# A hybrid gMLP and Mamba-2 block: transfers re-queued, PSUM split three and five, scan output normalised later, inverse roots four tiles at a time

## The chip, the core and the metric

The kernel runs on one core of one Trainium2 chip. Its engines work in parallel, each through its own instructions in order: TensorE (PE: matmuls and transposes), VectorE (DVE), ScalarE (ACT), GpSimd (POOL), and SyncE (SP), which here does nothing but issue DMA transfers, so that its instruction stream is one queue of transfers: one that waits holds up all behind it. The metric is the device time of a run in microseconds; lower is better.

## What is computed

One layer over 2048 latent tokens of width 1024 with 256 context tokens. All is fp32. Cut to what matters:

```python
def _rms(x):
    return x * rsqrt(mean(x * x, -1) + EPS)

def _token_mixer(h, ...):
    proj = h @ w_in                                   # u, v (1024 each), z (1024), xbc (1536), dt (32)
    xbc = silu(conv_centred(xbc)); xs, bm, cm = split(xbc)
    y = chunked_scan_forward(xs, dt, bm, cm) + chunked_scan_backward(...)   # chunks of 128 tokens
    y = y + xs * d_skip
    g = (y * silu(z)).reshape(b, l, 2, 512)
    ssd_out = _rms(g).reshape(b, l, 1024) * ssd_norm_w        # 2 groups
    u, v = split(gelu(proj[..., :2048]))
    v = _rms(v.reshape(b, l, 8, 128)) * gm_norm_w             # 8 heads
    mixed = einsum('hts,bcshd->bcthd', gm_ws, v) + gm_bs      # 128 x 128 per head and chunk
    return concat([u * mixed, ssd_out]) @ w_out

x = x + g1 * token_mixer(modulate(_rms(x) * norm1_w))
x = x + g2 * swiglu(modulate(_rms(x) * norm2_w))
return _rms(x) * final_norm_w
```

## The kernel before

Every large matmul is made of three, from operands split in a rounded high part and the low rest (mm3, L224 to L232). A unit is 24 such matmuls of 512 columns (8 slices of the inner dimension) into one PSUM buffer; there are 8 buffers of 512 fp32 columns, four in the pool psm (mmp, for units) and four in pss (smp, for all else).

The stages: modulation and the xbc projection of tokens 1024 to 2047 (block 1), then its v, u and z projections; the xbc projection of block 0; then, from about 750 us on, one long run of two streams. Its main stream is proj_z(0), proj_v(0), proj_u(0) (16 units each), then four output halves out_half (16 units each: block 1 with the gMLP half, block 0 with it, block 0 with the scan half, block 1 with the scan half). Its side stream is the backward scan's states of block 0 (ssd_bwd) and then ssd_y, the scan's output: 32 items, a chunk and a group each. For an item, y_load fetches a record (L687, two buffers of pool recp), y_seg the decay rows from fscr (L722, L723) and makes two masked matrices with ACT (L728, L730), DVE (L729, L731) and POOL (L733), y_out does the matmuls into three smp buffers (L750, L751, L753), a fourth for the state (L761), the sums on DVE (L756 to L767) with POOL's L766, multiplies by z (L771) and squares (L772). y_norm makes the inverse root of a chunk's two sums (newton, L238 to L243, 12 DVE instructions with L777, on 2 columns) and scales both halves on ACT (L780); y_store transposes them on PE (L787), copies (L789) and writes them to sscr. The function run takes SIDE = 2.74 steps of the side stream for one of the main stream, and a scheduler then sets the order of each engine from data, buffers and the written order. The last output half runs beside border, which prepares the feed-forward's operands: it reads x2scr (L1010), writes parts to cscr (L1020) and loads them back (L1044).

In the main stream proj_v makes gelu (gelu2: ACT L574, DVE L575, ACT L576, DVE L577), for each unit the inverse roots of its 4 heads (newton on 4 columns, with L635) and scales v (L637); mixing multiplies 4 units of v by gm_ws (L615), adds the bias (L617) and writes mscr (L620). proj_u multiplies gelu of u by that and writes gmscr (L602). out_half adds a unit to the residual (DVE L850), which it loads after the unit's matmuls (L849) from xT or x2scr and writes to x2scr at once (L851). load_mix loads operands of out_half, gmscr (L826) or sscr (L829), and splits them with ACT (L832) and DVE (L833). Weights come through L213 and are split by ACT (L216) and DVE (L217). The tiles tma (14) serve most of these, on both streams.

## Time and profile before

| what | value |
|---|---|
| median of 3 runs | 2999.11 us (2996.86 to 3005.99) |
| the profiled execution | 3001.86 us |
| its span, first to last instruction | 2999.7 us |
| PE busy | 2827.3 us, 94% |
| DVE, ACT, POOL busy | 2002.9, 1295.7, 633.1 us |
| mean granted clock of PE | 0.970 |
| DMA | 525.94 MB, mean 175 GB/s |

The profile is of one execution. Busy times are sums of instructions; a wait is put down to the engine and line that released it. The granted clock is a share of full speed: 1.0 is 2.4 GHz, 0.5 is 1.2 GHz, the two levels between which PE's clock changes here, so a value between is a mixture over the stretch.

### The profile page before, as it was taken

What the parts mean: (1) busy time and instruction counts of PE and PEld (TensorE: products, weight loads), DVE (VectorE), ACT (ScalarE), POOL (GpSimd) and SP (SyncE); (2) the same over time, 40 slices, a digit from 0 to 9 for tenths busy, and PEclk for the clock granted to TensorE, in tenths of its full rate; (3) what the DMA queues carried; (4) which work ended last, traced back from release to release, by engine and by line L of the source; (5) the groups of instructions that cost most, each with busy time, mean ns of one, the idle gap of its engine ahead of it and who ended that gap; (6) DMA issues with size and microseconds to landing.
All of it is one profiled execution on the core that took longest, in us unless ns stands there. A gap on an engine that the chain in (4) does not pass through costs nothing. (4 is left out here: it accounts for less than half of the span.)

```text
span 2999.7 us, 37193 instructions
## 1 busy us (share of the span) xinstructions
PE 2827.3 (94%) x12474; PEld 2253.5 (75%) x12474; DVE 2002.9 (67%) x3412; ACT 1295.7 (43%) x2387; POOL 633.1 (21%) x550
## 2 busy tenths in 40 slices
PE   7999999999998988999888799999999899999997
PEld 2788778878676767777767588888778788888885
DVE  6777966886788889778764555555776544445555
ACT  4444343344355556445452533333554333333443
POOL 3100000210131223222202244444110322221000
PEclk8999999999999999999999899999999999999998
DMA  5222567732754668877756544445766433224664
GB/s 222 88 91 88 186 217 231 261 120 82 231 168 148 194 203 254 242 244 235 210 163 221 172 158 159 160 158 165 256 224 206 142 106 106 96 100 131 226 193 157
DMA packets 295531, 525.94 MB, mean 175 GB/s; under 512 B 28838, under 2 KB 89638, under 8 KB 295340
## 3 DMA queue, kind: packets, MB, share of 16 engines
q1 hardware_dynamic: 295340, 523.57, 54.4%
q8 instruction: 98, 1.61, 0.2%
q14 instruction: 93, 0.76, 0.1%
HBM read 380.84 MB, written 142.62 MB: 175 GB/s over the span
## 5 line engine op out<-in xcount | busy, mean ns | idle before, releaser
L979 DVE TENSOR_TENSOR hl<-w,hl 128x1024 fp32r<-128x1024 f32 x286 | 371.9, 1306 | 308.9 <-ACT hl L978 127.1
L978 ACT CAST hl<-w 128x1024 fp32r<-128x1024 f32 x286 | 298.3, 1049 | 427.4 <-PE mmp L1094 121.5
L230 PE MATMUL mmp<-actt,whi 128*128 128x512 f32 x1120 | 458.2, 409 | 14.4 <-DVE t L850 8.0
L231 PE MATMUL mmp<-actt,whi 128*128 128x512 f32 x1120 | 448.5, 400 | 0.0
L232 PE MATMUL mmp<-actt,wlo 128*128 128x512 f32 x1120 | 445.8, 398 | 0.0
L1093 PE MATMUL mmp<-hl,hl 128*128 128x512 f32 x704 | 276.2, 392 | 5.5 <-DVE t L1201 2.3
L1095 PE MATMUL mmp<-hl,hl 128*128 128x512 f32 x704 | 276.0, 392 | 0.5 <-DVE hl L979 0.5
L1094 PE MATMUL mmp<-hl,hl 128*128 128x512 f32 x704 | 275.8, 392 | 0.0
L230 PEld LDWEIGHTS mmp<-actt,whi 128*128 128x128 f32 x1120 | 216.4, 193 | 65.9 <-DVE t L850 10.5
L231 PEld LDWEIGHTS mmp<-actt,whi 128*128 128x128 f32 x1120 | 216.4, 193 | 48.5 <-issue 5.5
L232 PEld LDWEIGHTS mmp<-actt,wlo 128*128 128x128 f32 x1120 | 215.6, 193 | 47.8 <-issue 1.7
L1093 PE MATMUL smp<-hl,hl 128*128 128x512 f32 x528 | 210.1, 398 | 16.5 <-ACT hl L978 16.5
L230 PE MATMUL mmp<-whi,actt 128*128 128x512 f32 x512 | 211.8, 414 | 0.0
L1094 PE MATMUL smp<-hl,hl 128*128 128x512 f32 x528 | 208.9, 396 | 0.0
L1095 PE MATMUL smp<-hl,hl 128*128 128x512 f32 x528 | 207.4, 393 | 0.0
L232 PE MATMUL mmp<-whi,actt 128*128 128x512 f32 x512 | 207.2, 405 | 0.0
L231 PE MATMUL mmp<-wlo,actt 128*128 128x512 f32 x512 | 205.8, 402 | 0.0
L985 DVE TENSOR_TENSOR t<-smp,t 128x512 f32<-128x512 f32 x88 | 60.5, 688 | 187.8 <-PE smp L1095 146.5
L1093 PEld LDWEIGHTS mmp<-hl,hl 128*128 128x128 f32 x704 | 132.4, 188 | 36.1 <-issue 2.7
L452 DVE SCALAR_TENSOR_TENSOR tma<-xin,cw,tma 128x512 f32<-128x512 f32 x192 | 144.3, 751 | 21.5 <-ACT tma L450 15.9
L985 POOL TENSOR_TENSOR w<-w 128x512 f32<-128x512 f32 x44 | 58.6, 1333 | 458.5 <-DVE hl L979 316.9
L733 POOL TENSOR_TENSOR tma<-tma 128x512 f32<-128x512 f32 x64 | 87.4, 1366 | 318.9 <-ACT tma L732 222.4
(267 smaller groups left out, 5875.7 us busy)
## 6 DMA issues: line engine op xcount, KB each, us to landing
w<-in_wall_dram SPq DMA_DIRECT2D x110, 512.0 KB, 4.1
ws<-in_wall_dram SPq DMA_DIRECT2D x104, 512.0 KB, 4.4
ascr<-t SPq DMA_DIRECT2D x154, 256.0 KB, 4.0
w<-ascr SPq DMA_DIRECT2D x154, 256.0 KB, 2.8
tma<-fscr SPq DMA_DIRECT2D x128, 256.0 KB, 5.8
w<-wscr SPq DMA_DIRECT2D x88, 256.0 KB, 3.5
t<-x2scr SPq DMA_DIRECT2D x74, 256.0 KB, 4.6
w<-in_wall_dram SPq DMA_DIRECT2D x66, 256.0 KB, 3.6
```

What stands on the lines that cost most here:

```text
L230: PE.matmul(ps, lhsT=lh, rhs=rh, start=(i == 0), stop=False)
L231: PE.matmul(ps, lhsT=lh, rhs=rl, start=False, stop=False)
L232: PE.matmul(ps, lhsT=ll, rhs=rh, start=False, stop=(i == n - 1))
L452: V.scalar_tensor_tensor(out=acc[:, :n], in0=raw[:, j:j + n], scalar=cw[:, ch, j:j + 1], in1=acc[:, :n], op0=ALU.mult, op1=ALU.add)
L733: G.tensor_tensor(out=A, in0=A, in1=fb, op=ALU.mult)
L978: S.copy(hi, x)
L979: eng.tensor_tensor(out=lo, in0=x, in1=hi.bitcast(F32), op=ALU.subtract)
L985: eng.tensor_tensor(out=o, in0=a, in1=b, op=ALU.add)
L1093: PE.matmul(ps, lhsT=hi[:, ms_], rhs=t[:, 0, :], start=first and k == 0, stop=False, skip_group_check=not first)
L1094: PE.matmul(ps, lhsT=hi[:, ms_], rhs=t[:, 1, :], start=False, stop=False, skip_group_check=not first)
L1095: PE.matmul(ps, lhsT=lo[:, ms_], rhs=t[:, 0, :], start=False, stop=k == 3, skip_group_check=not first)
```

## The change

Five things are changed together.

- *Transfer queue.* Writes of z, mixed v, u times v, and x2 are noted (behind) and issued only once the next unit's matmuls have been written (flush). out_half loads the residual tile of a unit while it writes out the one before. ssd_y asks for the record of item i + 2 before y_seg of item i + 1, from three buffers (rp3 is new), and for hscr at the head of y_seg, for group 1 into a tile of its own (hbp). The room for these comes from constants that are closed after the last xbc projection (cs2) and from NT2B, 3 to 2 (tiles of the second feed-forward matmul).
- *PSUM.* psm has three buffers and pss five; in ffn2 the first four banks are three mmp and one smp.
- *Scan output.* y_store transposes and writes the raw product, one item after y_out made it. y_rstd makes the inverse roots of four chunks and both groups at once (8 columns), transposes them and writes them to r3scr. load_mix loads them as rows over all partitions, and multiplies each of the 8 tiles by the norm weight and the row on DVE before the split.
- *v.* The inverse roots of four units are made at once (16 columns), and the four tiles are scaled then; mixing of the four before comes after the third unit instead of the second.
- *Feed-forward start.* Both inverse roots of block 1's residual are made at t = 1 of the first feed-forward stage; one was made within the last output half, one at t = 0. SIDE is 2.61; the side stream has 12 steps less.

The core of the diff:

```diff
-NT2B = 3
+NT2B = 2
+NPM = 3
-SIDE = 2.74
+SIDE = 2.61
...
-    psm = ctx.enter_context(tc.tile_pool(name="psm", bufs=4, space=PSUM))
-    pss = ctx.enter_context(tc.tile_pool(name="pss", bufs=4, space=PSUM))
+    psm = ctx.enter_context(tc.tile_pool(name="psm", bufs=NPM, space=PSUM))
+    pss = ctx.enter_context(tc.tile_pool(name="pss", bufs=8 - NPM, space=PSUM))
...
+    def behind(dst, src):
+        pending.append((dst, src))
+
+    def flush():
+        for dst, src in pending:
+            DMA.dma_start(dst, src)
+        pending.clear()
...
                     mm3(ps, [(hi[:, k * P:(k + 1) * P], lo[:, k * P:(k + 1) * P], hs[j][k][:, 0, :], hs[j][k][:, 1, :]) for k in range(KT)])
+                    flush()
                     t = gelu2(ps, tmp)
...
-                    DMA.dma_start(gmscr[h0 + i][:, ts_], t[:, :TB])
+                    behind(gmscr[h0 + i][:, ts_], t[:, :TB])
...
+                ms = sml()[:, :16]
                 for c in range(4):
...
-                    V.tensor_scalar(out=ms, in0=ms, scalar1=1.0 / P, scalar2=4 * EPS, op0=ALU.mult, op1=ALU.add)
-                    r = newton(ms, 4)
+                    vh.append(v)
+                    if c == 2 and prev is not None:
+                        mixing(*prev)
+                    if c < 3:
+                        yield
+                V.tensor_scalar(out=ms, in0=ms, scalar1=1.0 / P, scalar2=4 * EPS, op0=ALU.mult, op1=ALU.add)
+                r = newton(ms, 16)
+                for c, v in enumerate(vh):
...
+        hb = hbp[0].tile([P, TB], F32, name="hb", tag="hb") if g else tma()[:, :TB]
+        DMA.dma_start(hb, hscr[c][:, g * TB:(g + 1) * TB])
+        st["hb"] = hb
...
-        r = newton(ms, 2)
-        for g in range(2):
-            S.activation(ys[g], ys[g], AF.Copy, scale=r[:, g:g + 1])
+        r = newton(ms, 8)
         yield
...
+        ps = smp()
+        PE.transpose(out=ps[0:8, :P], in_=r, identity=ident)
+        t = tma()
+        S.copy(t[0:8, :P], ps[0:8, :P])
+        DMA.dma_start(r3scr[tb].rearrange("g (c x) -> (g c) x", x=P), t[0:8, :P])
...
+            if i + 2 < len(its):
+                st[i + 2] = y_load(rp, i + 2, *its[i + 2])
             if i + 1 < len(its):
                 yield from y_seg(st[i + 1], *its[i + 1])
...
+            if store is not None:
                 yield from y_store(*store)
...
+        if half == 1:
+            rb = [load_rb(r3scr[tb][g:g + 1, :], tma) for g in range(2)]
...
+                V.scalar_tensor_tensor(out=t[:, :TB], in0=t[:, :TB], scalar=sn, in1=rb[k // 4][:, :TB], op0=ALU.mult, op1=ALU.mult)
+                a = actt()
+                S.copy(a[:, 0, :], t[:, :TB])
+                V.tensor_tensor(out=a[:, 1, :], in0=t[:, :TB], in1=a[:, 0, :].bitcast(F32), op=ALU.subtract)
...
-                    t = tmp()
-                    DMA.dma_start(t[:, :TB], xT[m * P:(m + 1) * P, ts_] if half == 0 else x2scr[m][:, ts_])
+                    t = nxt.pop(0)
+                    if todo:
+                        fetch(*todo.pop(0))
+                    flush()
                     V.scalar_tensor_tensor(out=t[:, :TB], in0=ps, scalar=m_sb[:, 16 + m, 0:1], in1=t[:, :TB], op0=ALU.mult, op1=ALU.add)
-                    DMA.dma_start(x2scr[m][:, ts_], t[:, :TB])
+                    behind(x2scr[m][:, ts_], t[:, :TB])
```

What stands in the engines' orders at three places, before and after. In these rows a name carries the number of its buffer, and lines are those of the kernel that the rows are of.

PE in the u projection, before, from the end of a unit: the two transposes of a chunk (L787), then the matmuls of the next item (L750 to L761).

```order
L231 MATMUL mmp_10028<-actt_4807,whi_9442 128x512
L787 MATMUL smp_9788<-ident_225,tma_9350 128x128 x4
L787 MATMUL smp_9796<-ident_225,tma_9526 128x128 x4
L750 MATMUL smp_10003<-h01_2647,rec_sb_9609 128x512
L751 MATMUL smp_10004<-tma_9659,rec_sb_9609 128x512
L753 MATMUL smp_10002<-rec_sb_9609,tma_9615 128x64 x4
L753 MATMUL smp_10002<-rec_sb_9609,tma_9638 128x64 x4
L761 MATMUL smp_10018<-tma_9657,rec_sb_9609 128x512
```

After, in the output halves: the state's matmul of an item (L787), one transpose of the item before (L806), the next unit.

```order
L235 MATMUL mmp_10345<-actt_9536,whi_9653 128x512
L236 MATMUL mmp_10345<-actt_9536,wlo_9654 128x512
L787 MATMUL smp_10374<-tma_10139,rec_sb_9847 128x512
L806 MATMUL smp_10386<-ident_232,tma_10184 128x128 x4
L234 MATMUL mmp_10394<-actt_9501,whi_9937 128x512
L235 MATMUL mmp_10394<-actt_9501,whi_9937 128x512
L236 MATMUL mmp_10394<-actt_9501,wlo_9938 128x512
```

The transposes stood in pairs, on tiles that ACT had scaled; they stand singly now, on tiles that DVE wrote.

DVE in the u projection, before: L575 and L577 are the two gelu steps that read a unit's PSUM buffer (mmp), L601 the product with v, L238 to L243 the inverse root, L756 to L765 the scan's sums.

```order
L575 SCALAR_TENSOR_TENSOR tma_9688<-tma_9688,mmp_9663 128x512
L238 TENSOR_SCALAR sml_9696<-sml_9336 128x2
L756 TENSOR_TENSOR tma_9725<-smp_9713,eac_474 128x512
L239 TENSOR_SCALAR sml_9696<-sml_9696 128x2
L575 SCALAR_TENSOR_TENSOR tma_9775<-tma_9775,mmp_9750 128x512
L577 SCALAR_TENSOR_TENSOR tma_9688<-tma_9688,mmp_9663 128x512
L241 TENSOR_TENSOR sml_9697<-sml_9696 128x2
L764 TENSOR_TENSOR tma_9725<-tma_9725,tma_9511 128x512
L601 TENSOR_TENSOR tma_9688<-tma_9688,tma_9661 128x512
L242 SCALAR_TENSOR_TENSOR sml_9697<-sml_9697,sml_9336 128x2
L765 TENSOR_TENSOR tma_9725<-tma_9725,smp_9712 128x512
L243 SCALAR_TENSOR_TENSOR sml_9696<-sml_9697,sml_9696 128x2
```

After: gelu is L590 and L592, the product L617, the scan's sums L782 to L793, its matrices L758, a weight's low part L221.

```order
L590 SCALAR_TENSOR_TENSOR tma_9131<-tma_9131,mmp_9105 128x512
L758 SCALAR_TENSOR_TENSOR tma_9078<-tma_9078,acs_479,tma_9079 128x128
L782 TENSOR_TENSOR tma_9150<-smp_9138,eac_481 128x512
L758 SCALAR_TENSOR_TENSOR tma_9078<-tma_9078,acs_479,tma_9079 128x128 x3
L592 SCALAR_TENSOR_TENSOR tma_9131<-tma_9131,mmp_9105 128x512
L789 TENSOR_TENSOR h01_2607<-h01_2607,smp_9153 128x512
L617 TENSOR_TENSOR tma_9131<-tma_9131,tma_9103 128x512
L790 TENSOR_TENSOR tma_9150<-tma_9150,hb_8851 128x512
L590 SCALAR_TENSOR_TENSOR tma_9189<-tma_9189,mmp_9163 128x512
L791 TENSOR_TENSOR tma_9150<-tma_9150,smp_9137 128x512
L221 TENSOR_TENSOR wlo_9318<-ws_9315,whi_9317 128x1024
L793 TENSOR_TENSOR tma_9150<-tma_9150,hb_8851 128x512
```

Before, the second unit's first step (mmp_9750) stands ahead of the first unit's last (mmp_9663); after, a unit is done with before the next begins, and the narrow instructions are gone from between.

The SP queue in the last output half, before: the residual's load (L849), its write (L851), border's writes (L1020).

```order
L849 DMA t2_14188<-x2scr4_165 128x512
L1020 DMA cscr6_2_193<-t2_14153 128x512
L1020 DMA cscr7_2_201<-t2_14103 128x512
L851 DMA x2scr4_165<-t2_14188 128x512
L1020 DMA cscr4_2_209<-t2_14196 128x512
L849 DMA t2_14226<-x2scr5_166 128x512
L851 DMA x2scr5_166<-t2_14226 128x512
```

After: load L878, write L584, border's writes L1069, a weight L1104.

```order
L878 DMA t2_13653<-x2scr4_172 128x512
L584 DMA x2scr2_170<-t2_13567 128x512
L584 DMA x2scr3_171<-t2_13605 128x512
L1104 DMA w4_13911<-in_wall_dram 128x1024
L1069 DMA cscr3_2_212<-t2_13624 128x512
L1069 DMA cscr5_2_204<-t2_13664 128x512
L878 DMA t2_13701<-x2scr5_173 128x512
L1069 DMA cscr6_2_200<-t2_13666 128x512
L1069 DMA cscr7_2_208<-t2_13616 128x512
L1069 DMA cscr4_2_216<-t2_13709 128x512
L878 DMA t2_13739<-x2scr4_172 128x512
L584 DMA x2scr4_172<-t2_13653 128x512
```

Before, the load of a unit's tile stood behind the write of the unit before; after, it stands ahead of it, by one or two units.

## Rows read from the trace of the kernel before

**Rows 1.** The page, engine busy time and share of the span.

```profile
PE 2827.3 (94%) x12474; PEld 2253.5 (75%) x12474; DVE 2002.9 (67%) x3412; ACT 1295.7 (43%) x2387; POOL 633.1 (21%) x550
```

**Rows 2.** Windows, one row for each stretch named in the prediction.

```profile
core 0: us, PE busy (x) PEld busy (x) DVE busy (x) ACT busy (x) POOL busy (x), PEclk, DMA share, GB/s
860.00:1028.00 168.00, 148.72 (x701) 118.03 (x700) 148.42 (x444) 97.82 (x312) 35.74 (x30) 0.95 0.52 159
1028.00:1152.60 124.60, 111.76 (x502) 85.90 (x501) 100.89 (x219) 70.77 (x168) 38.71 (x29) 0.96 0.70 223
1152.60:1555.00 402.40, 369.31 (x1628) 290.23 (x1629) 305.35 (x640) 199.41 (x459) 95.37 (x79) 0.94 0.74 227
1555.00:1662.00 107.00, 94.54 (x375) 73.68 (x374) 51.68 (x74) 36.65 (x53) 17.05 (x11) 0.94 0.63 199
1662.00:1700.00 38.00, 19.35 (x63) 13.20 (x64) 25.82 (x33) 20.92 (x31) 8.97 (x7) 0.73 0.64 226
1700.00:2999.70 1299.70, 1263.81 (x5482) 1034.29 (x5481) 734.90 (x807) 502.85 (x640) 339.07 (x225) 0.99 0.49 160
```

**Rows 3.** Waits of PE, whole program: us in total, times, longest.

```profile
PE smp L787 <- ACT tma L780: 34.5, 9, 8.4
PE smp L1093 <- ACT hl L978: 16.5, 1, 16.5
PE mmp L230 <- DVE t L850: 8.0, 6, 3.0
PE smp L787 <- DVE tma L757: 5.5, 1, 5.5
```

**Rows 4.** The same wait in 1028 to 1152.6, then in 1152.6 to 1555.

```profile
PE smp L787 <- ACT tma L780: 6.6, 2, 4.9
PE smp L787 <- ACT tma L780: 19.8, 5, 8.4
```

**Rows 5.** Waits of ACT and of the SP queue in 795 to 1640.

```profile
ACT tma L728 <- DMA tma<-fscr: 126.2, 47, 7.2
...
SPq L687 <- POOL tma L766: 80.7, 24, 11.3
SPq L851 <- DVE tma L850: 66.6, 35, 5.6
```

**Rows 6.** DVE by line and shape; 128x4 in 860 to 1028, others 795 to 1640.

```profile
L243 DVE SCALAR_TENSOR_TENSOR sml<-sml 128x4 f32<-128x4 f32 x48 | 10.4, 217 | 0.7
...
L833 DVE SCALAR_TENSOR_TENSOR actt<-xin,vec,actt 128x512 fp32r<-128x512 f32 x32 | 22.6, 746 | 1.7 <-ACT actt L832 1.7
L242 DVE SCALAR_TENSOR_TENSOR sml<-sml 128x2 f32<-128x2 f32 x48 | 13.7, 286 | 0.7
```

**Rows 7.** Timeline of the last half: start us, us, engine, line.

```profile
1643.91 0.32 SPq L851 DMA_DIRECT2D x2scr<-t  x1
1645.48 0.45 SPq L849 DMA_DIRECT2D t<-x2scr  x1
1650.02 0.75 DVE L850 SCALAR_TENSOR_TENSOR t<-mmp,m_sb,t 128x512 f32<-128x512 f32 x1 [3.73 <-DMA t<-x2scr]
1650.80 0.32 SPq L851 DMA_DIRECT2D x2scr<-t  x1
```

**Rows 8.** Timeline at the feed-forward's start, queue and PE.

```profile
1679.14 0.33 SPq L851 DMA_DIRECT2D x2scr<-t  x1
...
1683.11 0.79 PE L1093 MATMUL smp<-hl,hl 128*128 128x512 f32 x1 [16.53 <-ACT hl L978]
```

**Rows 9.** Timeline of PE and DVE in the u projection.

```profile
1051.20 0.39 PE L230 MATMUL mmp<-actt,whi 128*128 128x512 f32 x1
1055.96 0.39 PE L230 MATMUL mmp<-actt,whi 128*128 128x512 f32 x1
1058.47 0.68 DVE L577 SCALAR_TENSOR_TENSOR tma<-tma,mmp 128x512 f32<-128x512 f32 x1
1059.20 0.50 PE L230 MATMUL mmp<-actt,whi 128*128 128x512 f32 x1 [2.40 <-DVE tma L577]
```

More of the change, by code (lines that the diff above doesn't have):

```diff
@@ L131 @@
     rscr = [tc.dram_tile([1, TB], F32, name=f"rscr{i}") for i in range(4)]
+    r3scr = [tc.dram_tile([2, TB], F32, name=f"r3scr{i}") for i in range(4)]
     r2scr = [tc.dram_tile([1, TB], F32, name=f"r2scr{i}") for i in range(4)]
@@ L394 @@
     tot = cst.tile([P, NT, 32], F32, name="tot")
-    halo = cst.tile([P, 12, 2], F32, name="halo")
+    halo = cs2.tile([P, 12, 2], F32, name="halo")
     def dt_block(c0, stat):
@@ L645, in proj_v @@
         yield
+    zdone = [0]
     def proj_z(blk, hs):
@@ L710, with y_load @@
     hv = lambda ap: bc(ap.rearrange("p (a o) -> p a o", o=1), HD)
-    def y_load(rp, c, g):
-        return {"rc": load_rec(rp, c, g, True)}
+    hbp = []
+    def y_load(pools, i, c, g):
+        return {"rc": load_rec(pools[i % 3 == 2], c, g, True)}
     def y_seg(st, c, g):
@@ L839, in out_half, with fetch @@
         pend = None
+        nxt = []
+        def fetch(m, j):
+            t = tmp()
+            ts_ = slice((blk * 2 + j) * TB, (blk * 2 + j + 1) * TB)
+            DMA.dma_start(t[:, :TB], xT[m * P:(m + 1) * P, ts_] if half == 0 else x2scr[m][:, ts_])
+            nxt.append(t)
+        todo = [(m0 + i, j) for m0 in range(0, 8, 2) for j in range(2) for i in range(2)]
+        fetch(*todo.pop(0))
         for m0 in range(0, 8, 2):
@@ L855, in out_half @@
                     if half == 1:
-                        acc[j] = sq_acc(acc[j], t[:, :TB], last_acc if last_acc and j == 1 and m == 0 else tmp)
+                        acc[j] = sq_acc(acc[j], t[:, :TB], last_acc if last_acc and m == 0 else tmp)
                         if m == 7:
                             pend = (acc[j], r2scr[blk * 2 + j], tmp)
-                            if j == 1:
-                                if last is None:
-                                    rstd_store(*pend)
-                                else:
-                                    last.append(pend)
+                            if last is not None:
+                                last.append(pend)
+                                pend = None
+                            elif j == 1:
+                                rstd_store(*pend)
                                 pend = None
@@ L959 @@
     late = []
-    accp = ctx.enter_context(tc.tile_pool(name="accp", bufs=1, reuse_waits="tile"))
+    accp = ctx.enter_context(tc.tile_pool(name="accp", bufs=2, reuse_waits="tile"))
     def acc1():
@@ L1165, in ffn1 @@
                 stage_y(t)
-            if blk == 0 and t == 0:
-                rstd_store(*box.pop())
+            if box and t == 1:
+                for b in box:
+                    rstd_store(*b)
+                box.clear()
             if blk == 0 and t % 2 == 1:
@@ L1214, in ffn2 @@
             if i == 0:
-                bank[p] = bank[1] if p in (6, 7, 4) else bank[5] if p == 3 else [mmp() if p == 1 else smp() for _ in range(4)]
+                bank[p] = bank[1] if p in (6, 7, 4) else bank[5] if p == 3 else [mmp() if p == 1 and m < NPM else smp() for m in range(4)]
             hi, lo = rdy.pop(n)
```

95 lines of the change are left out of this document (47 added, 48 removed).

## The prediction

> **What bounds the kernel now.** I read the page's engine shares first: TensorE (PE) is busy 2827.3 us of the span, 94% [rows 1], so time can only come from what is left to it: idle time, and time at a low clock. Then I cut the program where the changed code runs and read both per stretch [rows 2]. The edits lie in 860 to 1700 us; after 1700 PE is busy 1263.81 of 1299.7 us at clock 0.99 and little is to be had. For each stretch I take idle (length less PE busy) plus clock loss (length times one less the clock; a little too much, since it also counts time in which PE did nothing):
>
> - 860 to 1028, v projection (16 units of 24 matmuls): 19.3 + 8.4 = 27.7 us
> - 1028 to 1152.6, u projection (16 units): 12.8 + 5.0 = 17.8 us
> - 1152.6 to 1555, three output halves (48 units): 33.1 + 24.1 = 57.2 us
> - 1555 to 1662, the last output half (16 units): 12.5 + 6.4 = 18.9 us
> - 1662 to 1700, start of the feed-forward: 18.7 + 10.3 = 29.0 us
>
> Together 150.6 us. No edit that leaves PE's work alone can give more than about that here.
>
> Next, who is waited for [rows 3]. The largest wait is that of the transposes of the scan output (L787) for ACT's normalising copies (L780): 34.5 us in 9 waits. L787 also waits 5.5 us for DVE L757, which frees a PSUM buffer. Then 16.5 us once at the feed-forward's start, and 8.0 us for output buffers that DVE L850 has not yet freed. A gap costs twice: in the 38 us in which the wait of 16.53 us falls [rows 2, 8], the granted clock is 0.73, so PE ran part of it at the lower of its two levels, 1.2 instead of 2.4 GHz, after standing idle; in the last stretch, which has few gaps, it is 0.99. Last, why ACT is late: it waits 126.2 us for the rows of fscr, and the queue that loads them (SP, in order) stands 80.7 us before the record load L687, whose two buffers POOL still reads, and 66.6 us before the x2scr write L851, whose data DVE has not made [rows 5]. So the side stream is late because writes and a short pool hold up its loads, and PE, in order too, pays for it at L787.
>
> **The change part by part.** *Normalisation out of the scan.* Each of 16 chunks had a narrow inverse root on DVE and two copies on ACT (L780) before the two transposes. Now the transpose takes the raw product, and 4 inverse roots of 8 columns serve 4 chunks each. On PE's order the transpose of an item now stands behind the next item's matmuls, and its input is one DVE multiply, made a whole item earlier. The 34.5 us of waits for L780 lose their cause. What is late next at that place is DVE itself (L757, L756, h), and the fifth PSUM buffer of that pool takes most of it. On DVE the 128x2 rows [rows 6] with their siblings (six rows, 48 + 48 + 48 + 16 + 16 + 16 instructions) sum to 53.2 us; a quarter of the instructions is left, 13.3 us at the same duration, a saving of 40 us. In return load_mix gets one multiply for each of 32 tiles at L833's 0.746 us [rows 6]: 24 us more on DVE, in the stretch 1400 to 1700. Net 16 us less.
>
> *Four tiles of v at once.* The 128x4 rows [rows 6] with their siblings (six rows) sum to 37.7 us in 860 to 1028; a quarter is left, if 16 columns cost what 4 do, as 2 and 4 columns do (286 ns against 217 ns, no dearer for the wider): 28 us less of DVE's 148.4. The price: v's last multiplies come 4 units together, and mixing is moved one unit later, to cover that. This stretch is DVE's: 148.4 of 168 us [rows 2]. After it DVE has some 114 us (28 of v, 6 of the scan's share), PE's own floor is 168 - 27.7 = 140 us, and PE becomes the bound. I take **22 us** of 27.7. The v projection of the other block (before 779 us) has the same edit but PE stands hardly idle there: zero. The Trainium skill (Perfetto Trace Analysis, Optimizing Scalar/DVE Operations) says that every DVE instruction pays about 60 ns for data access on SBUF and that grouping helps a saturated engine. The narrow rows agree with it, at more than that figure; by 60 ns alone an estimate for the 144 instructions saved would be 9 us instead of 28, and the sum 5 to 10 us worse.
>
> *u projection.* L787's waits for L780 there are 6.6 us [rows 4] of the 12.8 idle; with the clock they caused I take **12 us** of 17.8, before the cost of the PSUM split, below.
>
> *Three output halves.* Most idle time there is L787's, 19.8 us for L780 alone [rows 4] of 33.1, and the largest of the rest is its 5.5 us for L757. Against taking all: DVE is busy 305.4 of 402.4 us and loses only about 5 net there; the floor of PE is 345 us, so DVE would stand at 87%, and some waits will come back as waits for DVE. I take **40 us** of 57.2.
>
> *Queue order.* Writes of z, v, u and x2 are held until the next unit's matmuls are written out, the residual tile is fetched a unit ahead, records have three buffers and are asked for an item earlier, hscr has a buffer of its own. In the last half this cuts a loop that the timeline shows [rows 7]: the write goes out at 1643.91, only then the next load at 1645.48, DVE L850 stands 3.73 us until it has landed, then the write at 1650.80. A turn is 6.9 us, a unit of PE's 24 matmuls 5.45 us (its first and last L230 stand at 1051.20 and 1055.96 [rows 9], seven turns of 0.68 us, and there are eight). Fetching ahead takes the load out of it. I take **12 us** of 18.9, and of the next stretch **15 us** of 29.0: PE stood 16.53 us until 1683.11 for a split of a tile that the queue loaded only behind the last write at 1679.14 [rows 8]; that write waited on the same loop. It will not vanish, since 12 loads still stand behind the last write. The cost: a held write keeps its tile a unit longer, and the fetch one more, out of the same 14 tiles; against that the scan keeps one product where it kept up to three. I price that at zero, 0 to 10 us.
>
> *PSUM three and five.* A unit may now start when the unit three before it is freed, not four. The bound: at 1059.20 PE waited 2.40 us for L577's release; the unit before had begun at 1051.20 [rows 9], and with three buffers it would have had to wait for the same release, 7.95 us. I went through PE's unit starts and DVE's releases from 803 us on: there are three such clumps in the u projection (8.8, 3.2 and 8 us at worst) and three in the output halves (4, 6 and 6.5 us), some 36 us; two smaller ones before 779 us make 44. At the other end it is zero: the lag arises since DVE takes two units at once (in DVE's order before, shown in the section on the change, the second unit's L575 stands ahead of the first's L577, with newton's instructions between), and the new order takes them one after the other. I take **20 us**, nearer the middle, since no row shows the new lag. The feed-forward's banks (three and one for the first four, then four) are as many as before: zero.
>
> *Rest.* NT2B 3 to 2 leaves 14 tiles for a peak that I count at 14: zero, 0 to 8 us. Both last inverse roots go to t = 1 of the feed-forward: 1 us, below what I can tell. The multiplies at the head of the last half stand before PE's first units: 8 of 0.75 us, **3 us**, 0 to 6.
>
> The sum: 22 + 12 + 40 + 12 + 15 = 101 gained, 20 + 3 lost: 78 us. The profiled execution took 3001.86 us, 2.8 over the median of the runs; 2999.1 - 78 gives **2921 us**.
>
> **The rivals.** *DVE takes over.* If the waits at L787 only move to DVE, which is 75 to 88% busy there, the gain is DVE's own saving and the queue's: 28 + 6 in the v and u stretches, half of the 40, and 20 at the end, less 23: 51 us, 2948; at worst 25 us, 2974. For it: rows 2. Against it: ACT's 126.2 us for fscr [rows 5] stand in front of DVE's L729 on the same tiles, so part of DVE's lateness is the queue's.
>
> *All of it.* Three buffers cost nothing and PE comes within 30 us of its floor: 2999 - 120 = 2879. For it: the even new order.
>
> *Slower: three PSUM buffers decide.* If DVE's lag behind PE stays what it was, 44 us of waits come, in gaps of up to 8 us, each with a low clock behind it: with half as much again, 66 us. It decides from the point at which the rest gives less than that; with L787's waits merely exchanged for it (gain 45 us): 3020. The Trainium skill (Perfetto Trace Analysis, Optimization Strategy) says that a gap that repeats on the engine that should be saturated can mean too few buffers. The two stalls on L577 with four buffers agree; by that rule taking one away makes it worse.
>
> *The change does not reach.* The queue's waits are exchanged for waits on free tiles and only the narrow DVE work goes: 2999 - 10 = 2989 to 2999.
>
> **How the numbers follow.** Forecast (2895 to 2945) 0.50; DVE takes over (2945 to 2988) 0.23; all of it (2860 to 2895) 0.14; does not reach (within 0.3%) 0.05; slower 0.08. A measurement of this kernel tells about 0.3% (9 us) from no change. So faster 0.87, same 0.05, slower 0.08. The range from 2872 to 2980 leaves out the upper end of the second case, the lower of the third, and the last two.
>
> **What would show it.** Right: L787's successor waits under 8 us in all; PE idle in the scan's stretches falls by half, the clock there to 0.98; the v stretch is about 20 us shorter; DVE L850's wait for x2scr is gone in the last half; the wait at the feed-forward's start is under 8 us. Wrong: waits of PE's main matmuls for the gelu's second DVE step or L850's successor above 30 us (three buffers), or DVE above 92% in the scan's stretches with PE still idle (DVE).

## The result and the profile after

The changed kernel takes 2977.35 us (median of 4 runs, 2974.7 to 2980.2), the kernel before 2997.99 beside it: a ratio of 0.9931, interval 0.9906 to 0.9956. That is 21 us less where 78 were forecast; the direction is right, the time lies at the upper end of the range, the size is off by more than three times.

In the profiled execution (2980.2 us, span 2978.4) the page has, against [rows 1]:

```profile
PE 2815.9 (95%) x12478; PEld 2252.8 (76%) x12478; DVE 1977.8 (66%) x3012; ACT 1272.8 (43%) x2360; POOL 637.6 (21%) x550
```

PE's idle time (span less busy) went from 172.4 to 162.5 us, its busy time fell by 11.4. To see where, both spans are cut at the same work in PE's own order: at the first matmul of block 0's z projection, at that of the last output half, at that of the feed-forward, and behind the feed-forward's first 96. Windows of the kernel before, then of the changed one (columns as in rows 2):

```profile
0.00:735.44 735.44, 699.26 (x3223) 548.59 (x3223) 546.59 (x1028) 316.51 (x608) 76.04 (x152) 0.98 0.50 161
735.44:1549.60 814.16, 744.96 (x3312) 579.20 (x3311) 639.17 (x1467) 413.94 (x1050) 191.97 (x156) 0.95 0.67 207
1549.60:1657.49 107.89, 96.61 (x388) 76.09 (x386) 52.11 (x76) 39.02 (x57) 17.05 (x11) 0.94 0.62 202
1657.49:1705.90 48.41, 28.58 (x100) 19.93 (x101) 30.80 (x38) 28.94 (x41) 13.02 (x9) 0.79 0.59 201
1705.90:2999.70 1293.80, 1257.91 (x5457) 1029.66 (x5455) 734.20 (x806) 497.31 (x634) 335.01 (x222) 0.99 0.49 161
```

```profile
0.00:738.28 738.28, 698.78 (x3222) 550.86 (x3222) 535.10 (x884) 317.52 (x608) 74.22 (x152) 0.98 0.49 160
738.28:1540.06 801.78, 739.52 (x3316) 577.26 (x3315) 609.26 (x1192) 387.86 (x1016) 198.61 (x156) 0.95 0.69 212
1540.06:1640.10 100.04, 90.41 (x388) 73.27 (x386) 69.23 (x98) 42.83 (x65) 18.31 (x12) 0.95 0.76 248
1640.10:1675.98 35.88, 24.55 (x98) 18.83 (x96) 28.03 (x33) 22.10 (x35) 11.67 (x8) 0.86 0.55 195
1675.98:2978.40 1302.42, 1262.62 (x5461) 1032.59 (x5459) 736.20 (x807) 502.44 (x638) 334.76 (x222) 0.98 0.49 160
```

The second rows are the scan's stages, that is the scan beside z, v, u and three output halves: 12.4 us shorter, PE idle 69.2 us before and 62.3 after, the clock 0.95 in both. Little of the forecast's main gain is there. The last half is 7.9 us shorter, the feed-forward's first 96 matmuls are 12.5 us shorter (idle 19.8 to 11.3, clock 0.79 to 0.86). The first row is 2.8 us longer and the last 8.6.

Within the second rows, v, u and the three output halves, before and after:

```profile
859.95:1006.08 146.13, 128.02 (x592) 102.05 (x590) 128.56 (x379) 86.72 (x278) 33.32 (x28) 0.94 0.48 146
1006.08:1152.56 146.48, 132.47 (x612) 101.88 (x610) 120.76 (x283) 81.87 (x201) 41.12 (x31) 0.97 0.71 226
1152.56:1549.60 397.04, 363.95 (x1605) 285.76 (x1605) 300.67 (x634) 194.60 (x453) 95.37 (x79) 0.94 0.74 226
```

```profile
864.91:1003.55 138.64, 125.79 (x597) 100.58 (x595) 106.24 (x236) 82.69 (x273) 31.98 (x27) 0.95 0.52 150
1003.55:1149.03 145.48, 130.49 (x616) 102.58 (x614) 119.25 (x230) 75.53 (x192) 42.87 (x33) 0.97 0.77 235
1149.03:1540.06 391.03, 361.70 (x1600) 283.53 (x1600) 291.46 (x566) 179.43 (x435) 101.84 (x79) 0.94 0.75 230
```

So v gives 7.5 us, u 1.0, the three halves 6.0, and z, the rest of the row, takes 2.1 us more.

Who PE waits for in 754 to 1566, the largest (us in total, times, longest), against [rows 3]:

```profile
PE smp L819 <- DVE sml L247: 22.9, 4, 8.3
PE smp L631 <- DMA gw<-in_gmw_dram: 13.2, 6, 6.2
PE mmp L234 <- DVE tma L592: 9.2, 2, 8.0
PE mmp L234 <- DVE tma L895: 8.7, 1, 8.7
PE smp L787 <- DVE h L789: 5.6, 1, 5.6
PE smp L779 <- POOL tma L762: 4.1, 2, 2.9
```

The 34.5 us for the normalising copies are gone, as forecast. In their place stand four waits of a new small transpose (L819) for the chain of inverse roots right ahead of it, which I overlooked; the mixing's weights (L631), 1.6 us before; main buffers, of which there are three (L234); and waits behind the load's bursts of VectorE steps (L787 once, and L895, below). At the feed-forward's start the largest wait is 8.24 us where [rows 8] had 16.53:

```profile
PE mmp L1144 <- DVE hl L1028: 9.3, 2, 8.2
```

And the side stream, against [rows 5]: ScalarE's wait for the broadcast row sums is nearly what it was. DVE, with 25 us less to do, waits longer behind ScalarE for the same loads (56.7 us in 38 before, at L729 for L728). The SyncE queue still stands before the held writes (the three last rows, whole program).

```profile
ACT tma L757 <- DMA tma<-fscr: 117.9, 44, 6.8
```

```profile
DVE tma L758 <- ACT tma L757: 74.0, 39, 5.7
```

```profile
SPq L584 <- DVE tma L895: 63.4, 19, 8.5
SPq L584 <- DVE tma L617: 60.8, 25, 9.8
SPq L584 <- DVE tma L679: 46.1, 18, 6.5
```

Single executions of one kernel differ here by 6 to 10 us, so a trace is read for its waits, and times are compared as ratios to the kernel before, measured beside each kernel.

### The profile page after: what moved, and what is told of

Same layout as the page of the kernel before. It is cut to its first block, busy times and chain, and to the rows that moved or that the text cites. A ratio compares the mean times of both kernels' runs of the same rounds, so it can differ in the third digit from the quotient of the medians.

```text
span 2978.4 us, 36719 instructions
## 1 busy us (share of the span) xinstructions
PE 2815.9 (95%) x12478; PEld 2252.8 (76%) x12478; DVE 1977.8 (66%) x3012; ACT 1272.8 (43%) x2360; POOL 637.6 (21%) x550
## 5 line engine op out<-in xcount | busy, mean ns | idle before, releaser
L234 PE MATMUL mmp<-actt,whi 128*128 128x512 f32 x1120 | 456.1, 407 | 24.9 <-DVE tma L592 15.4
L234 PEld LDWEIGHTS mmp<-actt,whi 128*128 128x128 f32 x1120 | 214.6, 192 | 74.9 <-DVE tma L592 17.6
L234 PE MATMUL mmp<-whi,actt 128*128 128x512 f32 x512 | 211.1, 412 | 2.4 <-DVE tma L679 2.4
L1144 PEld LDWEIGHTS mmp<-hl,hl 128*128 128x128 f32 x704 | 133.7, 190 | 38.9 <-DVE hl L1028 10.2
L1142 PEld LDWEIGHTS mmp<-hl,hl 128*128 128x128 f32 x704 | 133.5, 190 | 38.4 <-ACT t L1167 4.2
```

Source lines behind the costliest of these rows:

```text
L234: PE.matmul(ps, lhsT=lh, rhs=rh, start=(i == 0), stop=False)
L1142: PE.matmul(ps, lhsT=hi[:, ms_], rhs=t[:, 0, :], start=first and k == 0, stop=False, skip_group_check=not first)
L1144: PE.matmul(ps, lhsT=lo[:, ms_], rhs=t[:, 0, :], start=False, stop=k == 3, skip_group_check=not first)
```

## First experiments: the new waits one by one

Theory A: the forecast gain was given back in the new waits; each taken away brings its time. Theory B: something under them sets the pace, and a wait taken away comes back elsewhere.

**Late roots.** The roots' transpose stands after the next item's output and transposes.

```diff
-        r = newton(ms, 8)
-        yield
-        ps = smp()
-        PE.transpose(out=ps[0:8, :P], in_=r, identity=ident)
...
             if store is not None:
                 yield from y_store(*store)
+            if root is not None:
+                y_root(*root)
```

> The changed kernel with one thing moved: the transpose that turns the inverse roots of a token block (four times in the scan) is no longer issued right behind their chain of eleven small VectorE steps, but after the next item's output and transposes, some 20 us later. Theory A (the gain was given back in new PE waits): the four waits of the small transpose, 5.33, 5.86, 8.27 and 3.46 us, are gone, three of them certainly (the last token block's has least work left to hide it), nothing takes their place, and the stretches at the lower clock behind them are shorter: 2977 minus 18 to 30, so 2947 to 2959 us. Theory B (the scan's stages last as long as the side stream's chain of loads, ScalarE and VectorE steps lets them; PE's waits only move): the waits of that line go too, but PE waits elsewhere for VectorE or the side stream by as much: 2970 to 2980 us.

2970.84 us, 0.9919 (0.9905 to 0.9933): some 4 us, not told apart from the changed kernel. The waits of that line for the chain are nearly gone (1.1 us of 22.9); PE's waits on main buffers behind the load's burst rose:

```profile
PE mmp L234 <- DVE tma L903: 21.1, 3, 11.7
PE smp L631 <- DMA gw<-in_gmw_dram: 18.8, 8, 8.5
```

**PSUM four and four.** (The expectation calls the old wait the state product's; it was that of the transposes of the scan's output.)

```diff
-NPM = 3
+NPM = 4
```

> The changed kernel with four PSUM buffers for the main products and four for the scan's, as before the change, the rest as changed. Theory A: the waits for a main buffer (15.4 us in 4 at the gelu's second step, 8.7 us in 1 at the output's step) go, but the state product's wait of the kernel before (34.5 us in 9) comes back, since it stood on the fourth small buffer; balance 0 to +15 us, 2977 to 2992. If the normalisation step that held the small buffers is gone with the change anyhow, the wait does not come back and it gains 10 to 20 us: 2957 to 2967. Theory B (side stream decides): within 5 us, 2972 to 2982.

2979.23 us, 0.9945 (0.9930 to 0.9961): level with three and five. The main-buffer waits mostly go, and the transposes wait for buffers that DVE L782 frees, 16.5 us in 5.

**v tile by tile again.**

```diff
-                ms = sml()[:, :16]
...
+                    r = newton(ms, 4)
```

> The changed kernel with the inverse roots of v taken tile by tile again (four newton chains of 4 columns in place of one of 16, mixing behind the second tile), the rest as changed. Theory A: the grouping took some 13 us of small VectorE steps out of each v stage (two of them) without shortening it, since the mixing's loads came late and the last tile's chain now stands ahead of four multiplies; undoing it costs 0 to 8 us: 2977 to 2985. Theory B (VectorE's load decides in the scan's stages): the small steps are back, 12 to 26 us slower: 2989 to 3003.

2975.79 us, 0.9933 (0.9921 to 0.9945): nothing. The narrow steps are back on DVE (1336 instructions in the scan's stages for 1192) and the time is the same. In this trace v takes 146.97 us (138.64 with the grouping) and u 138.01 (145.48): what the grouping gains in v is lost again in u.

**Writes at once.**

```diff
     def behind(dst, src):
-        pending.append((dst, src))
+        DMA.dma_start(dst, src)
```

> The changed kernel with the writes of the main stream's results issued at once again (not behind the next product), the prefetch of the output's operand kept. Theory A: each write blocks the one DMA queue until its VectorE step is done, 1 to 4 us each, and with it the loads behind; what the reordered queue brought is 8 to 25 us, so 2985 to 3002 us. Theory B: the queue has slack, since PE waits mostly for VectorE: within 6 us, 2971 to 2983.

2988.81 us, 0.9980 (0.9968 to 0.9991): 15 us of the 21 hang on the held writes.

**The load's burst.** In the changed kernel DVE has this before the last half (start us, us):

```profile
1551.24 2.07 DVE L858 SCALAR_TENSOR_TENSOR xin<-xin,vec,tma 128x512 f32<-128x512 f32 x3
1553.22 1.89 DVE L861 TENSOR_TENSOR actt<-xin,actt 128x512 fp32r<-128x512 f32 x3
1555.03 0.74 DVE L895 SCALAR_TENSOR_TENSOR tma<-mmp,m_sb,tma 128x512 f32<-128x512 f32 x1
```

Rows like the first two stand without a gap from 1534.7 on, 20 us of them (16 multiplies and 16 differences), and only then comes L895, which frees a main buffer; PE stood 8.72 us for it. Taken in quarters between products:

```diff
-               early(out_half(0, 1, s0), 16, 2, lambda: [load_mix(2, 1), load_mix(3, 1)], s1)), 1),
+               early(out_half(0, 1, s0), 16, 4, quarters(2, 1, s1), None)), 1),
```

> The changed kernel with the mixers' operand loads (16 tiles ahead of each output half) taken in four quarters, one between each two products, instead of all 16 at one place; nothing else changed, and the last half's load begins four products ahead in place of two. In the changed kernel the 32 VectorE steps of such a load (16 multiplies of 0.68 us and 16 differences of 0.62 us, 21 us) stand in a row twice, and the output's steps behind them: PE waited 8.72 us at 1555 and 5.60 us at 1411 there, at three main buffers. Theory C (my step for this load, 3 us, was mis-sized: it is a burst that stops the buffers): those two waits go and the stretches at the lower clock behind them: 2975 minus 10 to 20, so 2955 to 2965 us. Theory B (a wait that goes comes back at another place): within 5 us, 2970 to 2980.

2986.3 us, 0.9974 (0.9961 to 0.9987): 13 us slower. The 8.72 us became three waits of 4.1, 2.7 and 1.4 us, the 5.60 us wait is gone, and the idle time of the scan's stages is 66.7 us (62.3 in the changed kernel). Why it is slower than the changed kernel I could not settle.

**All three repairs at once** (weights of the mixing a group ahead in four buffers, too).

```diff
-                gw = sp.tile([P, 2, P], F32, name="gw", tag="gw", bufs=2)
+                gw = sp.tile([P, 2, P], F32, name="gw", tag="gw", bufs=4)
...
-                prev = (hh, j, vh)
+                prev = (hh, j, vh, gw_load(hh))
```

> The changed kernel with three repairs at once: the inverse roots' transposes late, the operand loads in quarters, and the mixing's weights loaded one group of four tiles ahead into four buffers. The waits they aim at are 22.9, 14.3 and 13.7 us in the changed kernel. Theory A/C (the forecast gain was given back in these three): 2975 minus 25 to 50, 2925 to 2950 us. Theory B: late roots brought 4 us of their 22.9, and in the same proportion all three bring 9: 2960 to 2970.

2976.45 us, 0.9937 (0.9922 to 0.9952): the changed kernel's time. Taking away the waits aimed at, 51 us, brought nothing: in its trace PE waits for other DVE steps instead. Theory A falls.

## The parts alone

**Normalisation alone on the kernel before:** `y_store` per item, `y_rstd`, the multiply in `load_mix` and SIDE 2.61, nothing else.

```diff
-            S.activation(ys[g], ys[g], AF.Copy, scale=r[:, g:g + 1])
...
+            if g == 1 and c % 4 == 3:
+                yield from y_rstd(c // 4, ms)
```

> The kernel before with the scan's normalisation part alone (ScalarE's scaling of the two halves gone, each half transposed by itself, roots of four chunks at once, multiplies in the output projection's load; the side stream's rate 2.61 as in the changed kernel); four and four PSUM buffers, the old queue, v tile by tile. My forecast gave this part most of its 52 us in the output halves and part of v and u, since the transposes' wait for the scaling (34.5 us in 9) goes. Forecast's theory: 2997 minus 30 to 50, 2947 to 2967 us. Theory B (another step of the same chain is late next, and the load's burst takes its share): minus 0 to 10, 2987 to 2997.

3013.36 us, 1.0065 (1.0048 to 1.0082): 19 us slower. The wait for the copies is gone, and the same transposes (now L780) wait for DVE:

```profile
PE smp L780 <- DVE tma L757: 19.2, 3, 8.6
PE mmp L231 <- DVE t L857: 10.9, 5, 5.1
```

**Queue alone on the kernel before.**

```diff
-                DMA.dma_start(x2scr[m][:, ts_], t[:, :TB])
+                behind(x2scr[m][:, ts_], t[:, :TB])
...
+                    if todo:
+                        fetch(*todo.pop(0))
+                    flush()
```

> The kernel before with the queue part alone (writes behind the next product, the output's operand one product ahead, the third record buffer and the backward state's own buffer with their loads issued earlier); normalisation, v and the PSUM split as before. Undoing the writes alone in the changed kernel cost 14 us. If the parts add up: 2997 minus 10 to 18, 2979 to 2987 us. If the queue only pays once the normalisation's chain is gone: within 5 of 2997.

2981.3 us, 0.9952 (0.9937 to 0.9967): 14 us faster, although the wait that I had taken for the cause is longer than before:

```profile
PE smp L811 <- ACT tma L804: 56.8, 11, 12.4
```

By the same cuts its scan's stages take 814.02 us, for 814.16 before: what the queue part gains lies in the last half and at the feed-forward's start.

**The changed kernel without the normalisation.**

```diff
+            S.activation(ys[g], ys[g], AF.Copy, scale=r[:, g:g + 1])
...
-            if g == 1 and c % 4 == 3:
-                yield from y_rstd(c // 4, ms)
```

> The changed kernel without its normalisation part (ScalarE scales each half in the scan again, the pairs are transposed behind it, the load multiplies by one vector only; side rate 2.74 as before): queue, v grouping and PSUM three and five stay. If the parts add up, the normalisation is dead weight (alone it cost the kernel before 19 us): 2976 minus 10 to 22, 2954 to 2966 us. If it pays only once the queue is reordered (the transposes' wait for the scaling was 56.8 us with the queue alone): slower than the changed kernel by 3 to 15, 2979 to 2991 us.

2997.06 us, 1.0003 (0.9992 to 1.0014): within the whole the normalisation is worth 21 us, alone it costs 19. The 21 us lie in the scan's stages, which take 821.17 us here and 801.78 in the changed kernel.

**v grouping alone on the kernel before.**

```diff
-                    r = newton(ms, 4)
...
+                r = newton(ms, 16)
```

> The kernel before with the v grouping alone (one newton chain of 16 columns for four tiles, mixing behind the third tile). My forecast's term for it lay in the v stretch, 22 us with the other parts' share, some 13 of it the small VectorE steps: 2996 minus 8 to 22, 2974 to 2988 us. The runs so far (undoing it in the changed kernel moved nothing) say 0: 2990 to 3002 us.

3004.86 us, 1.0030 (1.0018 to 1.0042): 9 us slower; PE's wait for the mixing's weights is 12.0 us where it was 1.6. The parts do not add up: 19 and 9 us lost and 14 gained alone, 21 gained together (three and five PSUM buffers were not run alone). Only the queue part keeps its worth: 14 us alone, 15 for its held writes in the changed kernel.

**The multiply on GpSimd, with late roots.**

```diff
-                V.scalar_tensor_tensor(out=t[:, :TB], in0=t[:, :TB], scalar=sn, in1=rb[k // 4][:, :TB], op0=ALU.mult, op1=ALU.mult)
+                G.tensor_tensor(out=t[:, :TB], in0=t[:, :TB], in1=rb[k // 4][:, :TB], op=ALU.mult)
```

> The changed kernel with the roots' transposes late and the load's multiply by the roots on GpSimd (32 multiplies of VectorE less in the two bursts, ScalarE scaling and one VectorE step each as in the kernel before). Theory C (the burst in the load stops the main buffers): 4 us for the late roots and 8 to 15 for the burst, 2976 minus 12 to 19, 2957 to 2964 us. Theory B: as the late roots alone, 2968 to 2974.

2999.64 us, 1.0009 (0.9999 to 1.0019): 23 us slower than the changed kernel, 27 slower than with late roots alone. PE's wait for the scan's own step on GpSimd, 4.1 us in the changed kernel, is a part of it; the rest is not accounted for:

```profile
PE smp L779 <- POOL tma L762: 18.5, 6, 9.4
```

## What sets the pace

**PE freed from the scan's chain.**

```diff
-        PE.matmul(pb, lhsT=rc[:, R_C:R_C + P], rhs=hb, start=True, stop=True)
+        PE.matmul(pb, lhsT=rc[:, R_C:R_C + P], rhs=rc[:, R_X:R_X + TB], start=True, stop=True)
...
+            PE.transpose(out=ps[:, i * P:(i + 1) * P], in_=ident, identity=ident)
```

> The changed kernel with the operands of the scan's TensorE products and transposes in the output pass replaced by ones that are there long before (the record's own parts, the identity): as many TensorE instructions of the same shapes, but they no longer wait for the chain of loads, ScalarE, VectorE and GpSimd steps of their item; the output is not the reference's. All other work stays. It shows the most that any rearrangement of those waits can bring. Theory A (these waits are what the scan's stages lose): TensorE's 72 us of idle time in the scan's stages fall to 15 to 30, 2976 minus 40 to 60, 2916 to 2936 us. Theory B (TensorE then waits for buffers that the same chain's VectorE steps give back): 2976 minus 0 to 20, 2956 to 2976 us.

2973.53 us, 0.9928 (0.9914 to 0.9941): 1 us, not told apart from nothing; the two intervals leave room for some 9. So what PE still waits for the scan's operands in the changed kernel, mainly 22.9 us at L819 and 4.1 at L779, is worth next to nothing. It does not price the waits that my main step took away: without that step the kernel is 21 us slower. In the trace (the fastest execution of this kernel, against the slowest of the changed one) PE's idle time in the scan's stages is 56.5 us (787.49 less 730.99); it waits for buffers and weights instead:

```profile
PE smp L631 <- DMA gw<-in_gmw_dram: 21.7, 5, 12.0
PE smp L787 <- DVE h L789: 12.1, 1, 12.1
PE mmp L234 <- DVE tma L592: 12.1, 3, 7.4
```

What hands out buffers is DVE in its fixed order, and what hands out weights is the one queue. Theory D1: late loads set the pace; D2: DVE's work does.

**Writes on GpSimd's queue.**

```diff
         for dst, src in pending:
-            DMA.dma_start(dst, src)
+            G.dma_start(dst, src)
```

> The changed kernel with the writes of the main stream's results issued on GpSimd's queue instead of SyncE's, at the same places; SyncE's queue, which stood 170 us before those writes for their VectorE steps (63.4, 60.8 and 46.1 us at line 584), keeps only loads and the scan's stores. Theory D1 (the one queue in order is what makes the loads late, and late loads are what the scan's stages lose): 2976 minus 15 to 30, 2946 to 2961 us. Theory D2 (VectorE's work in its fixed order is the limit, the queue only second): within 6 us of 2976.

2991.32 us, 0.9979 (0.9968 to 0.9990): 15 us slower. GpSimd shows 250 instructions and 248 us in the scan's stages, for 156 and 199: 94 more, at about half a microsecond each. This does not decide between D1 and D2, since it loads the engine that the scan's items also need.

**No row-sum loads.**

```diff
-            DMA.dma_start(fb, fscr[c // 4][:, o:o + TB].broadcast_to([P, TB]))
-            DMA.dma_start(bb, fscr[c // 4][:, o + 16 * P:o + 16 * P + TB].broadcast_to([P, TB]))
```

> The changed kernel without the 128 broadcast loads of the scan's row sums in the output pass; ScalarE and VectorE read the record's own parts in their place and the exponential takes scale 0, so as many steps of the same shapes run, without those loads and without the waits for them (117.9 us of ScalarE, 74.0 us of VectorE behind it); the output is not the reference's. Theory D1 (late loads): 2976 minus 30 to 60, 2916 to 2946 us. Theory D2 (VectorE's order and work): minus 0 to 12, 2964 to 2976 us.

2916.84 us, 0.9739 (0.9723 to 0.9755): 59 us less. The scan's stages in its trace (cut and columns as above):

```profile
736.52:1474.93 738.41, 721.14 (x3316) 565.47 (x3315) 609.49 (x1191) 384.12 (x1015) 200.56 (x156) 0.99 0.58 184
```

PE is idle 17.3 us where it was 62.3, with as much work on DVE. The waits of L819, L592 and L631 shrink to 7.2, 0.9 and 5.7 us without being touched. More goes with these loads than their lateness: the DMA share falls from 0.69 to 0.58, and the tiles wait for no load.

**Less DVE work.**

```diff
-                V.scalar_tensor_tensor(out=A[:, es], in0=rc[:, R_WB:R_WB + P], scalar=dt_sb[:, c, 16 + h:17 + h], in1=A[:, es], op0=ALU.mult, op1=ALU.add)
...
-        V.tensor_tensor(out=ya, in0=ya, in1=yb, op=ALU.add)
```

> The changed kernel without two of the scan's VectorE steps in the output pass: the backward weight's product (256 small steps of line 760, 93.5 us of VectorE time) and the addition of the skip term (32 steps, 22 us, with its 32 products on GpSimd); loads, waits on them and TensorE's work stay; the output is not the reference's. Theory D2 (VectorE's work, 75 to 80 per cent busy in these stages and in fixed order, is the limit): 115 us less of it gives 2976 minus 30 to 60, 2916 to 2946 us. Theory D1: minus 0 to 12, 2964 to 2976 us.

2952.03 us, 0.9854 (0.9839 to 0.9868): 24 us for 106 us of DVE time and 40 us of GpSimd time taken away from the scan's stages; idle 47.0 us. Between the two expectations: the work of these engines counts, but the loads count for more than twice as much.

**Are the loads late, or dear?** They take 6.2 us to land (median, page) and are issued when ScalarE already wants them. Issued earlier, with one tile more for it:

```diff
+            if i + 2 < len(its):
+                st[i + 2]["f"] = y_fetch(*its[i + 2], 0)
             if store is not None:
                 yield from y_store(*store)
...
-NTMA = 14
+NTMA = 15
```

> The changed kernel with the row-sum loads of the scan's output pass issued earlier: those of an item's first half ahead of the store before it, those of the second half together with the item's other loads; one buffer more for it (15 of the common tiles, the small ones narrowed to make room). Same loads, same work. Theory D1 (the loads are issued when ScalarE already wants them, and it waits out their way, 117.9 us in 44): a third to two thirds of the 59 us that leaving them out brought, 2936 to 2958 us. Rival (their transfers, 33.5 MB, and their issue slots are what costs, wherever they stand; or the buffers they hold longer stop others): 2970 to 2985 us.

> The changed kernel with the fifteenth common tile alone, loads where they were: the control to the run before. Both theories: within 6 us of 2976, unless the common tiles are what holds the loads back; then 2960 to 2970 us.

> The changed kernel with the earlier row-sum loads, the fifteenth tile and the late transposes of the roots. If the late loads were what gave the late roots' 22.9 us back, both together bring more than the sum of each: the prefetch's gain and 8 to 20 us more, 2920 to 2948 us. If not: the prefetch's time minus 4.

Earlier loads 2960.01 us, 0.9890 (0.9872 to 0.9907); the tile alone 2977.47, 0.9945 (0.9930 to 0.9960); earlier loads and late roots 2954.59, 0.9861 (0.9843 to 0.9879). The scan's stages of the control, then of the two others:

```profile
737.88:1533.14 795.26, 735.58 (x3315) 574.37 (x3315) 607.06 (x1192) 388.63 (x1015) 200.65 (x156) 0.96 0.70 214
```

```profile
743.31:1517.22 773.91, 726.56 (x3315) 567.70 (x3315) 609.89 (x1192) 388.15 (x1016) 200.38 (x156) 0.98 0.71 220
```

```profile
743.00:1513.72 770.72, 732.04 (x3316) 572.09 (x3315) 606.04 (x1193) 387.93 (x1017) 197.78 (x156) 0.97 0.71 220
```

Idle 59.7, 47.4 and 38.7 us. Early issue brings 16 to 17 us over the control, with the same loads and the same work, so lateness is most likely part of it; the time lies in neither range that was expected, 2 us above that of D1. ScalarE's wait fell only from 121.9 us in the control to 105.2, DVE's behind it from 76.4 to 56.0:

```profile
ACT tma L757 <- DMA tma<-fscr: 121.9, 49, 6.6
```

```profile
ACT tma L762 <- DMA tma<-fscr: 105.2, 42, 7.5
```

How much of the other 42 us is lateness still, and how much transfers, issue slots and held tiles, is open. The last kernel beats both others: 1.4% below the kernel before, 0.7% below the changed one. Late roots bring 5 to 9 us there, for 4 in the changed kernel; that they pay more once the loads are early is not shown.

One rival stands beside all this. The scheduler makes a new order for every edited kernel. Of DVE's 1191 instructions in the scan's stages about 150 stand elsewhere in the order of the kernel without row-sum loads, and as many with early ones; 3 do in the control, 30 with PE freed (engine order in the traces, compared by operation and written tile). What the order does by itself no run separates.

## Why the prediction was wrong, step by step

- **The step that failed** is the gain in the scan's stages from taking L787's wait for L780 away: 22 + 12 + 40 us in v, u and three output halves, less 20 for PSUM, 54 in all. Measured were 7.5, 1.0 and 6.0, with 2.1 lost in z: 12.4 us. The wait went, as said; PE's idle time fell by only 7 us, since PE then waited elsewhere. I read the table of waits as a list of costs. The waits that stood in the old one's place are worth next to nothing (1 us with all operands ready, nothing for three repairs at once), while leaving out the row-sum loads brings 59 us and issuing the same loads earlier 16 to 17. The prediction had the likely cause in hand, ScalarE's 126.2 us for fscr [rows 5], and used it as an argument against a rival instead of asking which edit shortens it. None did: 117.9 us.
- **The step was not worth nothing.** Taking the normalisation out of the changed kernel costs 21 us, putting it alone into the kernel before costs 19. What a removed wait is worth depended on what else had been changed; why it loses alone is not shown.
- **v, 22 us.** Its stretch is 7.5 us shorter and DVE's work there fell from 128.56 to 106.24 us, but undoing the grouping moves nothing in the whole, since u gets shorter by as much, and alone it costs 9. That DVE was the bound there because it was 88% busy was the wrong inference. (The prediction's stretches were cut late for PE: 1028 lies 22 us behind its first matmul of u.) The Trainium skill (Perfetto Trace Analysis, Optimizing Scalar/DVE Operations) says that grouping can help if the engine is saturated; the trace agrees that fewer, wider steps take less of DVE's time, but DVE was not what limited the whole.
- **Last half and feed-forward start, 12 + 15 us:** 7.9 and 12.5 measured, near the forecast, with the load's multiplies in the first. The queue part alone gives 14, undoing the held writes takes 15. DVE's waits for x2scr there fell from 26.2 to 9.8 us, and PE no longer waits for them (8.0 us [rows 3]); one wait of 8.7 us behind the load's burst came in their place.
- **The roots at t = 1, put at 1 us:** of the 8.6 us lost in the last row 6.8 lie in the 192 matmuls after the first 96, where PE waits once and then runs a dozen matmuls at the lower clock (granted clock of that stretch 1.00 before, 0.93 after). The wait stands so (3.4 us) in three other kernels with both roots at t = 1, two of them with four main buffers, and not in the kernel before. NT2B, changed with it everywhere, is not separated from it. Before and after:

```profile
PE mmp L1093 <- DVE t L985: 1.0, 1, 1.0
```

```profile
PE mmp L1142 <- ACT t L1167: 3.5, 1, 3.5
```

- **PSUM, a loss of 20:** the waits came (15.4 us at the gelu's second step, 8.7 at L895; 6.4 and 8.0 before), but four buffers give nothing back, so the loss is not to be seen in the time. The rule of the Trainium skill (Perfetto Trace Analysis, Optimization Strategy) that a repeating gap can mean too few buffers is not borne out as to time: a buffer given back to one pool moves the gap to the other.
- **The load's multiplies, 3 us:** mis-sized as a wait. I counted eight multiplies, not 32 DVE steps in a row (and another such load before it, nearly in a row); PE waits 8.7 and 5.6 us behind them. Taken in quarters the load made the kernel 13 us slower, so what they cost is open.
- **A term was missing:** the root's transpose right behind its chain, 22.9 us of waits, worth some 4 us of time (late roots).
- **Signs named beforehand:** waits of L787's successor (L806) under 8 us: yes, none. PE idle halved in the scan's stages: no, 69.2 to 62.3. Clock to 0.98: no, 0.95. v stretch 20 us shorter: no, 7.5. DVE's wait for x2scr gone in the last half: no, 9.8 us. Wait at the feed-forward under 8 us: nearly, 8.24. Main-buffer waits above 30 us: no, 24.1. DVE above 92%: no, 76%.
- **The rivals.** "DVE takes over" ended at 2974, 3 us off, and is the nearest in kind: PE came to wait for DVE's order. But DVE's order waits for loads, which no rival said.

## What to carry to other kernels

A wait that stands at the end of a chain of loads, ScalarE and VectorE steps need not be a cost that an edit at its end gets back; look first at what starts the chain, and ask how long the chain would be if that wait were zero. The cheapest test is a kernel in which the waiting engine is fed operands that are already there: for that kernel it bounds what a whole class of edits can still bring. To see where time went, cut both traces at the same instruction of the engine that matters; cuts at another engine's steps move with its lag. Parts of a change to engines with fixed orders need not add up, in either direction (the normalisation: 19 us slower alone, 21 us faster in company), so a forecast by a sum of parts needs a check that one resource is not shared by all of them.

## What was unexpected of the hardware

Moving work to GpSimd, which is 21% busy, cost more than it saved both times: 32 multiplies (0.9919 with late roots alone to 1.0009) and 160 DMA issues, 94 of them in the scan's stages at about 0.5 us each (0.9931 to 0.9979). In the first PE's wait for the scan's own step on GpSimd rose from 4.1 to 18.5 us; in the second it hardly did (4.9 us), and the cause is open. The Trainium skill (Perfetto Trace Analysis, Optimizing Scalar/DVE Operations) warns that a move from DVE to GpSimd may not help because they share a port to SBUF; no run here separates that from GpSimd's order. And a load of 256 KB that the queue issues in 0.43 us took 6.2 us in the median to land, so one that is issued when its reader is free can make it wait some 6 us. That a broadcast is slower than other loads is not shown: in the scan's stages loads of the same size from gmscr and sscr took 4.9 and 4.7 us, those from mscr and x2scr 5.8 and 6.1.
